# Paired output: operands of the pairs in a pool of their own, the prompt tile under the global scale, the output weights' work in ten steps, the last pair's gating on VectorE

## The chip, the cores and the metric

The kernel runs on one core of one Trainium2 chip. A core has a matrix engine (TensorE, PE in the profile, with its weight loads under PEld), three engines for elementwise work (VectorE or DVE, ScalarE or ACT, GpSimd or POOL) and a queue processor that only issues transfers (SyncE or SP); POOL and ACT can issue transfers too. Every engine works through its own instructions in order and waits on the others by semaphores. Matrix products land in PSUM, in banks of 128 partitions by 512 floats; everything else lies in SBUF. Sixteen DMA engines carry all transfers; the profile names their queues q1 (issued by SP), q0 (by POOL) and q10 (by ACT).

The metric is the device time of one execution in microseconds, the median of several runs.

## The reference

One layer of a mixer is applied to two groups of tokens, 2048 sample tokens and 128 prompt tokens, with the same weights and D_MODEL = 1024:

```python
proj = jnp.einsum('btd,de->bte', xn, w_in)
...
br = jnp.stack([o_a, o_b, o_c], axis=2)                  # three branches, 512 wide each
pb = jnp.einsum('btnw,nwd->btnd', br, w_branch)
gt = jax.nn.sigmoid(gates.reshape(B, T, N_BRANCH, D_MODEL))
merged = jnp.einsum('btnd,btnd->btd', gt, pb)
return jnp.einsum('btd,de->bte', merged, w_out), s_f, s_b
...
h = h + gate * out
y = rmsnorm(h, final_g)
```

`gates` is the last part of the input projection (three times 1024 columns). Branch A is a bidirectional gated DeltaNet, branch B a spatial gating unit, branch C a Fourier mixing. The change touches only what comes after the branches: the merge (the sigmoid gates times the branch projections, summed over the three branches), the output projection by `w_out`, the gated residual and the final norm.

## The kernel before, in words

All matrix products are made with pairs of float16 numbers: a float32 operand is scaled by a power of two and split into a high part (an ACT copy with a scale) and a low part (a DVE operation that subtracts the high part from the scaled source), and a product takes three matmuls, hi by hi, lo by hi, hi by lo. All 17 tiles of 128 tokens lie in SBUF as `xh` and `xl`, normed and transposed, through the whole kernel.

**The merges.** `merge` (L1682) is called three times, for the branches n = 1, 2 and 0. It loops over eight blocks of 128 output channels (`db`), over two halves of the tokens (1024 sample tokens; 1024 sample tokens and the 128 prompt tokens), and over tiles of 512 (or 128) tokens. A tile has 24 matmuls for the gate and 12 for the branch projection; ACT takes the sigmoid (`sg`, L1713), DVE multiplies it by the branch sum (L1722, or L1719 in the first merge), and POOL adds the result to a row `mrow` that SP loaded from DRAM (`mD`) and that is stored back afterwards. For n = 0 the halves run the other way round, so that the prompt tokens come third and the last tile of the last block holds sample tokens 512 to 1023.

Weights for these blocks are read by SP into a buffer `wst` (two buffers in all), and converted in three steps: a Square on ACT that gives a norm, a scale from it (a small matmul and a few DVE operations), and the split. `weight_step` (L379) takes one step of the next conversion or begins another; two steps after one has ended it issues the next read. In the kernel before it is called once per tile, through `pace.tick`. `getw(2, 2)` at the start of a block makes sure that the block's gate weight and branch weight are ready and allows two more. `gate_rows` (L1746) works between them, a chunk per half block from the fourth block of the second merge to the fourth of the third: it loads pieces of `w_ada` into the same two `wst` buffers and sums them on DVE (`ada_sum`, L466), for the row of residual gates in DRAM (`gateD`).

In the third merge the output weights are prepared as well (`out_w` (L1806), blocks 0 to 3; `out_step` takes two steps per tile), and from block 4 on `quarters` (L1843) turns each finished pair of rows, the one of block `db - 4` and the one of `db`, into seven split operands for the output stage, which POOL stores into DRAM (`paD`, L1858). All of these are split under one global scale `ms_s`, which stands before the third merge begins; its inverse is `ms_i`.

**The output stage.** Two sample tiles at a time (`two_tiles`, L1984) are multiplied by `w_out` with seven products instead of eight, from the seven operands (tile `pa`, 1.8 MB) and four prepared sums of weights (`tw`, 1 MB each, which SP loads into the place of `xl`). The prompt tile is done first and by itself (`one_tile`, L1957). In the kernel before its operand is prepared after the third merge's prompt tile of the last block: `ahead_out` calls `single` (L1873), which loads the whole prompt column of `mD`, takes its own Square and scale, and splits it into `whi` and `wlo`; the residual gates for the prompt are scaled by that scale and the weights' scales (`inv8`).

The buffers `bwp` (branch weights), `big` (the branch operand `o16` and `mrow`) are closed when the merges end, and the pool `op` of the output stage (two `pa` tiles, the sample's gate row `gb`, `final_g` and small things) lies in their place. A third `pa` tile lies in the pool `orp`. `next_pair` (L1922) issues the loads of `pa`. The rows of x for the residual are loaded into the place of `xh`.

Each pair's rows get gate, residual, Square with a row sum (ACT), the norm and the final scale, and are stored. The last pair (`end`) does this in pieces, so that less is left when the last matmul ends: pieces of 512, 384 and 128 columns, with row sums joined in `summed_up` (L2033) and two powers on POOL (L2065, L2066).

**Order.** The engines' order in this part is not written by hand. A planner lists the instructions of each engine by the times at which it believes them to be ready, and, where several are ready, by their place in the program; `tc.high_priority()` moves some ahead, `tc.issue_after` holds some back.

## Time and profile before

| | us |
|---|---|
| three runs | 2177.23, 2179.75, 2179.76 |
| median of the runs | 2179.75 |
| the profiled execution, its own time | 2178.41 |
| its span, first to last instruction | 2174.7 |
| PE busy | 2085.2 |
| third merge | from about 1725 to 1995 |
| prompt tile (`one_tile`) on PE | 1996 to 2011 |
| eight pairs on PE | 2015 to 2162 |
| end of the span | 2174.7 |

All times in the tables and rows are counted from the span's start. A row of the timeline has the start, the duration, the engine with the line of the kernel, the operation, what it writes and reads, and, in brackets, how long the engine stood idle before it and which instruction released it. A row of the waits has the waiting instruction, the one that it waited for, the sum in us, how many times, and the longest. The line is that of the innermost helper: all matmuls are recorded at L241, all output splits at L1803 (ACT) and L1804 (DVE), and the weights' splits at L317 and L318, so rows are told apart by their tiles. "SPq" and "POOL DMA_DIRECT2D" rows are issues of transfers; the bytes land later.

### The profile page before, as it was taken

The numbers are of one execution on the slowest core, as the hardware profiler recorded it, in microseconds if no ns is written. First come the engines' busy times: TensorE is split into PE (matmuls) and PEld (weight loads), VectorE is DVE, ScalarE is ACT, GpSimd is POOL, SyncE is SP. The second block draws the span as 40 slices with busy tenths as digits, with TensorE's granted clock in tenths as the row PEclk, the third lists the DMA queues.
The fourth block names the chain that finished last, engine by engine and source line by source line (L and its number), as shares of the span: only waits on it lengthen the run. The fifth ranks groups of instructions, "written<-read, shape, count | busy, mean of one in ns | idle before, by whom it ended". The sixth has DMA issues, their size and how long they took to land. (4 is left out here: it accounts for less than half of the span.)

```text
span 2174.7 us, 42636 instructions
## 1 busy us (share of the span) xinstructions
PE 2085.2 (96%) x16122; PEld 1191.9 (55%) x16122; DVE 1368.0 (63%) x3099; ACT 1061.8 (49%) x2454; POOL 761.9 (35%) x939
## 2 busy tenths in 40 slices
PE   7999999999899999999899999899999999999997
PEld 4455444465455677777465555555555544444443
DVE  6657744389778798457655556665563565566344
ACT  5554744476555664444544446655553443443111
POOL 0321332232433432443122223354533243343455
PEclk9999999999999999999999999999999999999999
DMA  9526732277776743444755455867665554557652
GB/s 349 217 75 198 253 121 81 88 235 219 239 231 211 231 146 91 140 140 117 232 167 162 161 172 181 251 212 220 201 203 158 165 193 135 182 201 267 255 218 102
DMA packets 222925, 403.36 MB, mean 185 GB/s; under 512 B 39720, under 2 KB 109888, under 8 KB 219904
## 3 DMA queue, kind: packets, MB, share of 16 engines
q1 hardware_dynamic: 167648, 290.65, 42.0%
q0 software_dynamic: 15248, 65.95, 8.3%
q10 hardware_dynamic: 39824, 44.05, 6.0%
q8 instruction: 126, 2.06, 0.4%
q14 instruction: 79, 0.65, 0.1%
HBM read 258.26 MB, written 142.30 MB: 184 GB/s over the span
## 5 line engine op out<-in xcount | busy, mean ns | idle before, releaser
L241 PE MATMUL b<-xh,whi 128*128 128x512 f16 (+1 forms) x1920 | 650.2, 348 | 4.0 <-DVE sg L1443 2.7
L241 PE MATMUL b<-xl,whi 128*128 128x512 f16 (+1 forms) x1920 | 651.0, 348 | 0.0
L241 PE MATMUL b<-xh,wlo 128*128 128x512 f16 (+1 forms) x1920 | 650.2, 348 | 0.0
L241 PEld LDWEIGHTS <-whi 128*128 128x128 f16 x3872 | 353.3, 98 | 328.4 <-issue 13.3
L241 PEld LDWEIGHTS <-wlo 128*128 128x128 f16 x1936 | 189.7, 98 | 179.5 <-DVE wlo L1804 3.1
L241 PE MATMUL b<-big,bhi 128*128 128x512 f16 (+1 forms) x960 | 250.8, 347 | 7.1 <-ACT big L1677 3.7
L241 PE MATMUL b<-big,blo 128*128 128x512 f16 (+1 forms) x480 | 163.0, 347 | 1.4 <-DVE blo L318 1.4
L1723 POOL TENSOR_TENSOR mrow<-mrow,sg 128x512 f32<-128x512 f32 (+1 forms) x80 | 92.2, 1153 | 146.9 <-DVE sg L1722 113.1
L241 PEld LDWEIGHTS <-xh 128*128 128x128 f16 x1496 | 117.1, 98 | 31.0 <-issue 2.3
L241 PEld LDWEIGHTS <-bhi 128*128 128x128 f16 x960 | 86.2, 98 | 83.6 <-issue 7.6
L943 POOL TENSOR_TENSOR cy<-cy,raw 128x545 f32<-128x545 f32 (+1 forms) x48 | 63.8, 1356 | 183.7 <-ACT raw L942 183.7
L241 PEld LDWEIGHTS <-pa 128*128 128x128 f16 x684 | 66.8, 98 | 83.8 <-ACT xh L1952 3.9
L1713 ACT ACTIVATE sg<-b,winv 128x512 f32<-128x512 f32 (+1 forms) x120 | 73.9, 616 | 66.1 <-PE b L241 65.3
L1177 POOL COPY T<-ES 32x256 f16<-32x256 f16 x68 | 29.2, 429 | 195.9 <-DMA ES<-ei 180.0
L241 PE MATMUL b<-whi,xh 128*128 128x128 f16 x544 | 92.9, 219 | 2.2 <-DVE yT L1629 1.4
L1722 DVE SCALAR_TENSOR_TENSOR sg<-b,binv,sg 128x512 f32<-128x512 f32 (+1 forms) x80 | 53.3, 666 | 63.1 <-PE b L241 58.3
L241 PE MATMUL b<-whi,xl 128*128 128x128 f16 x544 | 92.9, 219 | 0.0
L241 PE MATMUL b<-wlo,xh 128*128 128x128 f16 x544 | 92.9, 219 | 0.0
L318 DVE SCALAR_TENSOR_TENSOR wlo<-wst,wsc,whi 128x1024 f16<-128x1024 f32 x52 | 72.6, 1397 | 28.3 <-ACT whi L317 28.2
L305 ACT ACTIVATE wlo<-wst 128x1024 f16<-128x1024 f32 x52 | 55.0, 1058 | 68.2 <-DMA wst<-in_w_blk_dram 62.6
L241 PE MATMUL b<-xl,pa 128*128 128x512 f16 x384 | 86.8, 379 | 0.0
L1284 POOL TENSOR_TENSOR skn<-skn,ed 128x512 f32<-128x512 f32 x34 | 38.7, 1138 | 122.6 <-DMA skn<-kv 118.7
(512 smaller groups left out, 4312.8 us busy)
## 6 DMA issues: line engine op xcount, KB each, us to landing
wst<-in_w_blk_dram SPq DMA_DIRECT2D x58, 512.0 KB, 4.6
pa<-pa POOLq DMA_DIRECT2D x16, 896.0 KB, 4.3
pa<-pa SPq DMA_DIRECT2D x8, 1792.0 KB, 7.1
qkv<-cy POOLq DMA_DIRECT2D x12, 1089.0 KB, 5.2
st<-br SPq DMA_DIRECT2D x48, 256.0 KB, 3.2
mrow<-mrg SPq DMA_DIRECT2D x16, 576.0 KB, 4.2
dc<-dec SPq DMA_DIRECT2D x17, 512.0 KB, 5.0
kq<-qkv SPq DMA_DIRECT2D x34, 256.0 KB, 5.0
```

The source lines that it names most:

```text
L241: newest[0] = PE.matmul(out, l, r, start=start, stop=stop, skip_group_check=reopened)
L305: w.squared = A.activation(w.lo, st, AF.Square, accum_out=ss)
L318: w.low = V.scalar_tensor_tensor(w.lo, st, s, w.hi, ALU.mult, ALU.subtract)
L943: G.tensor_tensor(y[:, c0:c1], y[:, c0:c1], raw[:, 1 + c0:1 + c1], ALU.mult)
L1177: G.tensor_copy(T16[rows(a0, b), :, :, b], ES[0:32, :, 2 * a0 + b, :, wT])
L1284: G.tensor_tensor(h3(kn_), h3(kn_), bc(ed[:, d, t, :], P), ALU.mult)
L1713: gated_[0] = A.activation(sg, ps, AF.Sigmoid, scale=gw.inv)
L1722: V.scalar_tensor_tensor(sg, ps, binv[:, 1:2], sg, ALU.mult, ALU.mult)
L1723: G.tensor_tensor(mr, mr, sg, ALU.add)
```

## The change

1. `mrow` moves from the pool `big` to a pool `mrp` of its own, and the pairs' operands from `op` to a pool `opa` that is opened ahead of `op`.
2. `weight_step` is called once more per tile in all three merges.
3. `out_w` gets a further yield behind each of its two Squares, so that a block's preparation has ten steps after its load, two for each of the five tiles.
4. `single` goes away. At the start of the last block of the third merge `prompt_rows` loads seven of the eight row blocks of the prompt column from `mD` and splits them under the global scale `ms_s`; the eighth is split straight out of `mrow` when its tile is done, and no longer stored.
5. `ahead_out` multiplies the output weights' scales by `ms_i` once, scales the prompt's gates by them, and loads and scales the sample's gate row `gb` there too, into a `wst` buffer. Before, `gb` was loaded and scaled after the merges.
6. After the merges the first `next_pair` stands ahead of the loads of `tw` in the program.
7. In the last pair, DVE instead of POOL does the additions of the residual (three of them) and the gating of `p1`; `gated`, which the last pair no longer calls, uses POOL always; the row sums' small steps (`summed_up`) are put behind the last addition.

`halves` is renamed `as_pair`.

```diff
+    mrp = pool(ms_, "mrp", 2)
...
-                mrow = sb(big, [P, hn], "mrow", bufs=2)
+                mrow = sb(mrp, [P, hn], "mrow")
...
+                    if n == 0 and t0 == NS and db == KT - 1:
+                        as_pair(p16[0][:, db, :], p16[1][:, db, :], mr, ms_s)
+                    weight_step()
                     if step is not None:
                         step(db)
                     pace.tick(tn * MT)
...
-                if n or db < 4:
+                if n:
                     (SY if first else G).dma_start(mD[db][:, h0:h0 + hn], mrow)
-                elif h0:
+                elif db < 4:
+                    G.dma_start(mD[db][:, h0:h0 + hn], mrow)
+                elif h0 and db < KT - 1:
                     G.dma_start(mD[db][:, NS:NTOK], mrow[:, NS - h0:NTOK - h0])
...
                 A.activation(wlo[:, :, cols_[i]], sts[i], AF.Square, accum_out=ss[:, i:i + 1])
             yield
+            yield
...
-    def single(t, hl, pl, tag):
-        mt = sb(pl, [P, KT, P], tag, bufs=2)
-        SY.dma_start(mt, mD[:, :, t * P:(t + 1) * P].rearrange("k p t -> p k t"))
-        ss = sb(orp, [P, 1], "mss")
-        with tc.high_priority():
-            A.activation(hl[1], mt, AF.Square, accum_out=ss)
-            s, inv = scales(ss, orp, "msc")
-            halves(hl[0], hl[1], mt, s)
-        return hl, inv
...
+    def prompt_rows():
+        mt = sb(wp, [P, KT, P], "wst", bufs=2)[:, 0:KT - 1]
+        SY.dma_start(mt, mD[0:KT - 1, :, NS:NTOK].rearrange("k p t -> p k t"))
+        p16.extend(sb(wp, [P, KT, P], n_, F16, bufs=4) for n_ in ("whi", "wlo"))
+        as_pair(p16[0][:, 0:KT - 1], p16[1][:, 0:KT - 1], mt, ms_s)

     def ahead_out(h0):
         if h0:
-            pre.append(single(16, [sb(wp, [P, KT, P], n_, F16, bufs=4) for n_ in ("whi", "wlo")], wp, "wst"))
-            inv8 = sb(orp, [P, KT], "inv8")
-            V.tensor_scalar(inv8, winv, pre[0][1], None, ALU.mult)
+            for _ in weights_out:
+                pass
+            V.tensor_scalar(winv, winv, ms_i, None, ALU.mult)
             for i in range(2):
                 gp.append(sb(ep, [P, 512], "sg", bufs=4))
                 SY.dma_start(gp[i], gateD[1:2, i * 512:(i + 1) * 512].to_broadcast([P, 512]))
-                scale_gate(gp[i], gp[i], inv8[:, 4 * i:4 * i + 4])
+                scale_gate(gp[i], gp[i], winv[:, 4 * i:4 * i + 4])
+            gp.append(sb(wp, [P, D], "wst", bufs=2))
+            SY.dma_start(gp[2], gateD[0:1, :].to_broadcast([P, D]))
+            scale_gate(gp[2], gp[2], winv)
...
         if db == KT - 1:
             for _ in gates:
                 pass
+            while wsteps:
+                weight_step()
+            prompt_rows()
...
+    opa = pool(ctx, "opa", 2)
     op = pool(ctx, "op", 2)
...
-            ready.append(operands(orp, 1) if i % 3 == 2 else operands(op, 2))
+            ready.append(operands(orp, 1) if i % 3 == 2 else operands(opa, 2))
...
-    summed_in(1, 2)
     next_pair()
-    gb = sb(op, [P, D], "gb", bufs=1)
-    fg = sb(op, [P, D], "fg", bufs=1)
-    SY.dma_start(gb, gateD[0:1, :].to_broadcast([P, D]))
-    summed_in(0, 3)
+    for q in (1, 2, 0, 3):
+        SY.dma_start(tw[:, q].rearrange("p j l k c -> p j (l k c)"), tD[q])
...
-            (V if end else G).tensor_tensor(hh[j][:, cs], hh[j][:, cs], gb[:, cs], ALU.mult)
+            G.tensor_tensor(hh[j][:, cs], hh[j][:, cs], gb[:, cs], ALU.mult)
...
-        G.tensor_tensor(hh[0][:, left], hh[0][:, left], xr[0][:, left], ALU.add)
+        (V if end else G).tensor_tensor(hh[0][:, left], hh[0][:, left], xr[0][:, left], ALU.add)
...
+        def gate_add(out, src, gate, other):
+            V.tensor_tensor(out, src, gate, ALU.mult)
+            return V.tensor_tensor(out, out, other, ALU.add)
+
         total(u2, X, u2)
-        gated(1, right)
-        V.tensor_tensor(u2, u2, gb[:, right], ALU.mult)
-        G.tensor_tensor(u2, u2, xr[0][:, right], ALU.add)
-        G.tensor_tensor(p1, p1, gb[:, left], ALU.mult)
-        G.tensor_tensor(p1, p1, xr[1][:, left], ALU.add)
+        gate_add(p1, p1, gb[:, left], xr[1][:, left])
+        gate_add(hh[1][:, right], hh[1][:, right], gb[:, right], xr[1][:, right])
+        piece(1, 0, right, G)
+        gate_add(u2, u2, gb[:, right], xr[0][:, right])
+        piece(0, 0, left, G)
         product(Y, pa, 2, summed(3), False)
-        piece(1, 0, right, G)
-        piece(0, 0, left, G)
-        summed_up(1, 0)
-        summed_up(0, 0)
...
-        summed_up(1, 1)
-        summed_up(0, 1)
-        summed_up(0, 2)
+        with tc.issue_after(sooner.ins):
+            for j, i in ((1, 0), (0, 0), (1, 1), (0, 1), (0, 2)):
+                summed_up(j, i)
```

More of the change, by code (lines that the diff above doesn't have):

```diff
@@ L1800, in hybrid_flow_kernel, with as_pair @@
     tmp = sb(orp, [P, D], "sums")
-    def halves(hi, lo, src, s):
+    def as_pair(hi, lo, src, s):
         A.activation(hi, src, AF.Copy, scale=s)
@@ L1824, in out_w @@
             for q in q4:
-                halves(whi[:, q, cols_[i]], wlo[:, q, cols_[i]], sts[i][:, q], s)
+                as_pair(whi[:, q, cols_[i]], wlo[:, q, cols_[i]], sts[i][:, q], s)
             yield
@@ L1831, in out_w @@
             slot = slots[:, (4 * j + q) % 3]
-            halves(slot[:, 0], slot[:, 1], out, s)
+            as_pair(slot[:, 0], slot[:, 1], out, s)
             G.dma_start(tD[q, :, j, :], slot.rearrange("p l k c -> p (l k c)"))
@@ L1920, in hybrid_flow_kernel @@
     ready = []
+    gb, fg = gp[2], sb(op, [P, D], "fg", bufs=1)
     def next_pair():
@@ L1957, in one_tile @@
     def one_tile(t, prepared, xr, hh):
-        (mh, ml), inv = prepared
+        mh, ml = prepared
         for i in range(2):
@@ L2038, in summed_up @@
                 V.tensor_scalar(q_[:, 0:1], q_[:, 0:1], 1.0 / D, EPS, ALU.mult, ALU.add)
+        def gate_add(out, src, gate, other):
+            V.tensor_tensor(out, src, gate, ALU.mult)
+            return V.tensor_tensor(out, out, other, ALU.add)
         total(u2, X, u2)
-        gated(1, right)
-        V.tensor_tensor(u2, u2, gb[:, right], ALU.mult)
-        G.tensor_tensor(u2, u2, xr[0][:, right], ALU.add)
-        G.tensor_tensor(p1, p1, gb[:, left], ALU.mult)
-        G.tensor_tensor(p1, p1, xr[1][:, left], ALU.add)
+        gate_add(p1, p1, gb[:, left], xr[1][:, left])
[3 more added lines that the diff above has]
+        piece(0, 0, left, G)
         product(Y, pa, 2, summed(3), False)
-        piece(1, 0, right, G)
-        piece(0, 0, left, G)
-        summed_up(1, 0)
-        summed_up(0, 0)
         with tc.high_priority():
-            V.tensor_tensor(hh[1][:, left], Y, gb[:, left], ALU.mult)
-            sooner = V.tensor_tensor(hh[1][:, left], hh[1][:, left], p1, ALU.add)
+            sooner = gate_add(hh[1][:, left], Y, gb[:, left], p1)
             piece(1, 1, left, V)
@@ L2057, in two_tiles @@
             with tc.high_priority(), tc.issue_after(sooner.ins):
-                V.tensor_tensor(hh[0][:, cs], Z, gb[:, cs], ALU.mult)
-                V.tensor_tensor(hh[0][:, cs], hh[0][:, cs], u2[:, cs.start - 512:cs.stop - 512], ALU.add)
+                sooner = gate_add(hh[0][:, cs], Z, gb[:, cs], u2[:, cs.start - 512:cs.stop - 512])
                 piece(0, i, cs, V if i == 2 else G)
-        summed_up(1, 1)
-        summed_up(0, 1)
-        summed_up(0, 2)
+        with tc.issue_after(sooner.ins):
+            for j, i in ((1, 0), (0, 0), (1, 1), (0, 1), (0, 2)):
+                summed_up(j, i)
         norms = sb(op, [P, 2], "norms", bufs=1)
@@ L2077, in hybrid_flow_kernel @@
     next_pair()
-    one_tile(16, pre[0], xr[0], hh[0])
+    one_tile(16, p16, xr[0], hh[0])
     for i, t in enumerate(firsts):
```

13 lines of the change are left out of this document (4 added, 9 removed).

## The prediction

> **What bounds the kernel now.** I read the page's first part, then the list of TensorE's waits, then the timeline around each wait that the edits touch. The page first (share of the span, instructions):
>
> ```profile
> span 2174.7 us, 42636 instructions
> PE 2085.2 (96%) x16122; PEld 1191.9 (55%) x16122; DVE 1368.0 (63%) x3099; ACT 1061.8 (49%) x2454; POOL 761.9 (35%) x939
> ```
>
> TensorE (PE) is busy for 96%, and the change removes no matmul that matters, so it can win only idle PE time: 89.5 us in all, most of it in stages that it does not touch. The list of PE's waits (us in total, times, longest) shows what is within its reach:
>
> ```profile
> PE b L241 <- DMA pa<-pa: 3.5, 1, 3.5
> ...
> PE b L241 <- ACT sg L1713: 2.9, 2, 1.7
> ...
> PE b L241 <- DVE wlo L1804: 2.6, 1, 2.6
> ...
> PE b L241 <- DVE blo L318: 1.4, 2, 1.2
> ...
> PE b L241 <- ACT bhi L317: 0.6, 1, 0.6
> ```
>
> The first and third are the passage from the last merge to the output stage; the others are the merges. The rest is the tail behind the last matmul. I cost these three places apart.
>
> **The passage.** The timeline (start, us, what; idle before it and its releaser in brackets):
>
> ```profile
> 1994.93 0.38 PE L241 MATMUL b<-big,blo 128*128 128x512 f16 x1
> ...
> 1996.24 3.58 DVE L1804 SCALAR_TENSOR_TENSOR wlo<-wst,msc,whi 128x1024 f16<-128x1024 f32 x1
> 1996.26 0.39 PE L241 MATMUL b<-wohi,whi 128*128 128x512 f16 x1 [0.96 <-ACT whi L1803]
> ...
> 1999.88 0.39 PE L241 MATMUL b<-wohi,wlo 128*128 128x512 f16 x1 [2.58 <-DVE wlo L1804]
> ...
> 2010.86 0.38 PE L241 MATMUL b<-wohi,wlo 128*128 128x512 f16 x1
> 2014.72 0.59 PE L241 MATMUL b<-wohi,pa 128*128 128x512 f16 x1 [3.48 <-DMA pa<-pa]
> ```
>
> The merge ends at 1995.3. The prompt tile's 48 matmuls wait for its conversion (whi, wlo). The first pair then waits for its operands `pa` until 2014.72. The change converts the prompt tile inside the last block (seven eighths from DRAM, the last straight from the row, no Square and no scale of its own), so both waits go: 0.96 + 2.58. At the pitch between neighbouring 128x512 matmuls (1996.49 to 1996.71, 0.216) the 48 take 10.4 us, and PE reaches the first pair at 2005.7. That is worth something only if `pa` is there. Who held it, in SyncE's (SP's) waits and its timeline:
>
> ```profile
> SPq L1926 <- DVE sums L1853: 10.4, 1, 10.4
> ```
> ```profile
> 1992.18 1.06 SPq L1930 DMA_DIRECT2D xl<-tw  x2
> 2003.87 0.37 SPq L1926 DMA_DIRECT2D pa<-pa  x1
> ```
>
> SP sat for 10.4 us until the last reader of mrow was done, because `pa` lies in a pool over the merge's buffers. With mrow and `pa` in pools of their own only the last merge matmul (1995.3) holds it, and the issue moves from 2003.9 to about 1995.4. That looks like the whole 9 us. But the transfers ahead of it decide. Issues from 1988 to 1994 (KB each, median us to landing), then `pa`'s own, then the bytes that moved from 1988 to 2008.8 and from 1988 to 2013.2 (packets, MB, share):
>
> ```profile
> xl<-tw SPq DMA_DIRECT2D x4, 1024.0 KB, 14.4
> xh<-in_x_sample_dram SPq DMA_DIRECT2D x3, 512.0 KB, 4.9
> xh<-in_x_prompt_dram SPq DMA_DIRECT2D x1, 512.0 KB
> ```
> ```profile
> pa<-pa SPq DMA_DIRECT2D x1, 1792.0 KB, 10.7
> ```
> ```profile
> q1 hardware_dynamic: 1194, 6.32, 80.1%
> ```
> ```profile
> q1 hardware_dynamic: 1712, 8.15, 83.8%
> q0 software_dynamic: 258, 1.62, 16.6%
> ```
>
> Four weights of 1.049 MB and four rows of 0.524 MB make 6.29 MB on SP's queue ahead of `pa`; with its 1.835 MB, 8.13. The queue had moved 6.32 by 2008.8 and 8.15 by 2013.2, and `pa` landed 10.7 us after 2003.87, at 2014.6, 1.4 us behind its last byte: the queue works in order and `pa` waited for bandwidth. An issue 8.5 us earlier, behind the same eight transfers, gains nothing.
>
> Could `pa` go ahead of them? Their target (xl, xh) comes free with the last gate matmuls, some 2.6 us before the branch matmuls that now hold `pa`. SP's order follows readiness, not the program: the x rows, later in the program than the weights, are issued among them. I take `pa` as last of the nine again.
>
> So the landing is set by bytes. The prompt's 0.5 MB load and gate row gb leave the stretch; the former only shared the engines before 1988. GpSimd's (POOL's) queue q0 carries the stores of the merge, 0.92 MB each; of its 1.62 MB, 0.70 were a store still open at 1988, and I let a third of them, 0.23, move sooner. The merge's last store comes earlier too, since VectorE (DVE) no longer spends 3.58 us on wlo ahead of it. It is issued at 2009.88 today; by the distance between the first two of these rows it will start 7.6 us behind the last sg, which can follow the merge's end at 1995.6,
>
> ```profile
> 1987.62 0.75 DVE L1722 SCALAR_TENSOR_TENSOR sg<-b,binv,sg 128x512 f32<-128x512 f32 x1 [1.67 <-PE b L241]
> ...
> 1995.26 0.72 POOL L1858 DMA_DIRECT2D pa<-pa  x1 [5.55 <-DVE msc L270]
> ...
> 2009.88 0.75 POOL L1858 DMA_DIRECT2D pa<-pa  x1 [0.84 <-DVE pa L1804]
> ```
>
> so at 2003, and its 0.92 MB now shares the engines with what stands ahead of `pa`. Net +0.69 MB at 0.42 MB/us (below) is **+1.6 us** at the start of the pairs; bounds -0.6 (store late) and +2.2 (all of the store, nothing freed). PE waits about 10 us in one piece instead of three. After the old wait it ran at half clock,
>
> ```profile
> 2004.00:2014.00 10.00, 7.24 (x33) 3.05 (x31) 3.75 (x4) 1.76 (x3) 3.68 (x3) 0.98 1.02 423
> ...
> 2014.70:2018.10 3.40, 3.38 (x9) 1.23 (x10) 0.04 (x1) 0.00 (x0) 0.79 (x2) 0.51 1.01 420
> ```
>
> (us, busy time of PE, PEld, DVE, ACT, POOL, clock, DMA share, GB/s), 1.7 us lost, and will again: no change.
>
> **The conversion's new place.** The last block gets an ACT copy of 128x896 (about 1.0 us by the 1.15 of 1024), a DVE operation of up to 3.1 (7/8 of 3.58), a 128x128 pair, gb's load and its POOL scaling (1.9 us, from the pairs' start). They lie beside 33 us of matmuls with DVE idle for 12: nothing. Without that cover the 3.1 us of DVE would keep a finished sum in PSUM and PE waiting for the bank. On SP the prompt's load now stands ahead of the last block's row loads; it waits for the row store of the block before, which POOL issues half a block (some 16 us) earlier, so nothing queues behind it. It takes one wst buffer and gb the other, when no weight is left to read. The last prompt row's store to DRAM, the Square, three scale steps and one 1-column matmul fall away beside other work; the renamed helper costs nothing.
>
> **The merges.** A second weight step per tile makes a weight's three steps end within the third tile of a block; today the branch weight's last step falls into the next block, and PE waits: blo 1.4 and bhi 0.6, **-2.0 us**. The two sg waits are another matter:
>
> ```profile
> 1836.59 3.25 DVE L466 SCALAR_TENSOR_TENSOR sg<-wst,scT,sg 128x256 f32<-128x256 f32 x8 [4.79 <-DMA wst<-in_w_ada_dram]
> ...
> 1839.87 0.33 SPq L282 DMA_DIRECT2D wst<-in_w_brb_dram  x1
> ...
> 1842.47 0.63 ACT L305 ACTIVATE blo<-wst 128x512 f16<-128x512 f32 x1 [10.76 <-DMA wst<-in_w_brb_dram]
> ...
> 1843.82 0.27 PE L241 MATMUL b<-big,bhi 128*128 128x128 f16 x2 [1.70 <-ACT sg L1713]
> ```
>
> A gate chunk holds one of the two wst buffers, SP's load of the branch weight waits for it, ScalarE (ACT) stands 10.76 us in its Square, and the sigmoid behind it starves PE. The new steps read further ahead (three tiles instead of one or two), but through the same two buffers, so I leave these 2.9. Bounds: -4.9 (both groups gone), and above as the slow rival. The output weights' ten steps in five tiles instead of eight in four move ACT's, DVE's and POOL's work and POOL's stores one tile later; no wait of PE on them stands in the list, and the cover is 7.8 us of matmuls (36 at 0.216) in each tile. Without it a conversion of two 128x1024 weights, four ACT operations of 0.7, would stand ahead of a sigmoid.
>
> **The tail.** Rows of the last pair:
>
> ```profile
> 2156.77 0.68 DVE L2000 TENSOR_TENSOR xh<-b,st 128x512 f32<-128x512 f32 x1
> 2157.37 0.68 DVE L2000 TENSOR_TENSOR st<-b,st 128x512 f32<-128x512 f32 x1
> 2157.97 0.68 DVE L1995 TENSOR_TENSOR xh<-xh,gb 128x512 f32<-128x512 f32 x1
> 2158.56 1.76 DVE L2042 TENSOR_TENSOR st<-st,gb 128x512 f32<-128x512 f32 x1
> 2162.24 0.15 DVE L2038 TENSOR_SCALAR part<-part 128x1 f32<-128x1 f32 x1 [1.92 <-ACT xh L2030]
> ...
> 2166.58 0.28 DVE L2059 TENSOR_TENSOR xh<-xh,st 128x128 f32<-128x128 f32 x1
> ```
> ```profile
> 2158.06 1.71 POOL L2045 TENSOR_TENSOR sg<-sg,xh 128x512 f32<-128x512 f32 x1
> ...
> 2161.41 1.27 POOL L2031 TENSOR_TENSOR xh<-xh,fg 128x512 f32<-128x512 f32 x1
> ```
>
> DVE stood 1.92 us in a row-sum step behind POOL's additions; the change puts those additions on DVE and the row-sum steps last. DVE then has, from 2156.5, eleven 512-wide operations at the pitch of 0.60 (2156.77 to 2157.37), about 1.0 for the 384-wide pair and 0.5 for the 128-wide: 8.1 us, last addition at 2164.6 instead of 2166.86, -2.2. Against that stands POOL: three multiplications (1.27, 1.27, 1.04) remain, and DVE's operations stretch beside POOL (1.76 against 0.68). I take one such block of 1.2: **-1.0**; bounds -2.2 and, with all three, +1.4. The Trainium skill, page SBUF — State Buffer, section Who interferes with whom, says that a DVE instruction with two SBUF inputs contends with a GpSimd instruction that reads SBUF and that the loser fully blocks; the 1.76 agrees. By that rule all three can block, and the tail would be +1.4.
>
> **Sum.** +1.6 - 2.0 - 1.0 = -1.4 against the profiled execution's 2178.41: 2177.0. The three runs' median is 1.34 above that execution, so I forecast **2178**. Less than 0.2% (4.4 us) can't be told from no change.
>
> **Rivals.**
> *`pa` first.* If SP takes `pa` ahead of the weights, it lands near 2001 and PE runs through: -9.0 of idle, -1.7 of half clock, -3.0 of the rest: -13.7, 2166. For it: `pa` stands first in the new program text. Against: order by readiness.
> *Merges and tail at their best*: -4.9, -2.2, +1.6: -5.5, 2174.
> *Every POOL operation blocks in the tail*: +1.6 - 2.0 + 1.4 = +1.0, 2181. For it: the 1.76 ended 0.55 behind POOL's 1.71; against: the 0.68 at 2157.97 fell between two POOL operations and paid nothing.
> *Slower: ACT stands behind weight reads in every block that has a gate chunk.* Eight have one (four of the second merge, four of the third), two stall now at 1.15 and 1.70. Earlier Squares wait for the same buffers; six more at 1.4 are +8.4, in all +7.0: 2187. It decides from the fifth. For it: ACT's 10.76; against: reads lead by more.
>
> **Chances.** Forecast 0.45, `pa` first 0.10, merges and tail at best 0.19, POOL in the tail 0.08, slower rival 0.18. Faster 0.29, same 0.53, slower 0.18. The range 2170 to 2186 leaves out `pa` first and the top of the slow rival; the forecast alone has -4.8 (-0.6 - 2.0 - 2.2) to +1.6 (2.2 - 2.0 + 1.4), 2175 to 2181.
>
> **What would show it.** Right: no PE wait on whi or wlo at the passage; `pa` issued near 1995 yet landing some 18 us later, PE waiting about 10 us for it; no PE wait on blo or bhi; ACT's long brb waits still there; fewer microseconds between last matmul and end. Wrong: `pa` issued ahead of the weights, or new PE waits in the merges.

## The result, and the profile after

The changed kernel takes 2170.99 us (median of 8 runs, 2164.11 to 2173.97) against 2181.52 for the kernel before on the same chip: ratio 0.9946, 95% interval 0.9930 to 0.9963. (All ratios are estimated from all runs of a group and are not quotients of the two medians.) Beside the last experiments it was timed again: 2173.27 against 2178.78, ratio 0.9975, interval 0.9960 to 0.9989. So it is faster, by some 5 to 12 us; the forecast was 2178 and "no change". That 2170.99 lies just inside the range of 2170 to 2186 is luck: the fastest rival in that range stood at 2174. Two runs far out of line, 12445.25 us of e6 and 4413.44 us of the kernel before beside e5 to e8, are left out of the ratios.

The profiled execution after took 2164.11 us. It is the fastest of its eight: the first merge starts at 1033.1 in it, and between 1033.1 and 1046.2 in the profiled executions of the kernels below that run the same matmuls ahead of it (all but e10, e11 and e15); the changed kernel itself, profiled twice, has both ends of that range. Those microseconds belong to no edit, so the stages are compared by their length.

Before, by windows (from the first sigmoid of each merge to the next; the merge's end to the first pair's first matmul; the rest. Length, then the busy time of PE, PEld, DVE, ACT and POOL, PE's clock, DMA share, GB/s):

```profile
1037.50:1399.00 361.50, 346.37 (x3100) 205.33 (x3100) 215.87 (x556) 182.99 (x442) 95.61 (x144) 0.99 0.60 186
1399.00:1728.50 329.50, 325.65 (x2629) 186.12 (x2628) 187.40 (x489) 171.85 (x465) 140.15 (x164) 1.00 0.64 200
1728.50:1994.93 266.43, 261.10 (x1436) 126.67 (x1434) 160.65 (x341) 113.65 (x192) 101.91 (x110) 1.00 0.52 177
1994.93:2014.72 19.79, 12.78 (x51) 5.00 (x50) 11.09 (x16) 4.35 (x6) 8.40 (x8) 0.91 1.01 401
2014.72:2174.70 159.98, 146.84 (x684) 66.80 (x684) 67.80 (x94) 24.98 (x47) 84.93 (x75) 0.96 0.50 187
```

The same windows after:

```profile
1033.10:1389.50 356.40, 347.85 (x3108) 207.20 (x3108) 214.58 (x560) 184.68 (x445) 99.84 (x144) 0.99 0.61 190
1389.50:1720.10 330.60, 324.76 (x2620) 186.30 (x2619) 194.55 (x489) 170.98 (x465) 137.69 (x163) 0.99 0.63 198
1720.10:1981.73 261.63, 260.76 (x1435) 126.52 (x1433) 159.54 (x330) 111.71 (x185) 101.30 (x112) 1.00 0.52 179
1981.73:2002.22 20.49, 12.33 (x50) 5.03 (x49) 8.79 (x16) 6.03 (x9) 6.34 (x6) 0.86 1.02 422
2002.22:2162.30 160.08, 147.44 (x684) 66.94 (x684) 68.83 (x99) 25.18 (x49) 75.31 (x69) 0.96 0.49 186
```

The first merge is 5.1 us shorter, the second about 1 longer, the third 4.8 shorter; passage and pairs, at which five of the seven edits aim, are 0.7 and 0.1 longer. PE's idle time (length less busy) falls in the first merge from 15.1 to 8.6 us and in the third from 5.3 to 0.9. In the second it rises from 3.9 to 5.8: PE has a new wait of 3.0 us for a sigmoid at 1710.08 (1.4 us when the change was profiled again, e14). That sigmoid stood on ScalarE behind a copy that waited for the load of a branch's rows (`st` from `br`); new waits of PE in the merges were one of the signs of being wrong that the prediction named. ScalarE's waits for weight reads fall with PE's idle time. In the waits of the whole run (sum, times, longest), `blo` is written by the Square of a branch weight and `wlo` by that of a gate weight; before:

```profile
ACT wlo L305 <- DMA wst<-in_w_blk_dram: 62.6, 27, 6.8
ACT blo L305 <- DMA wst<-in_w_brb_dram: 56.3, 18, 10.8
```

and after:

```profile
ACT wlo L305 <- DMA wst<-in_w_blk_dram: 51.0, 25, 6.8
ACT blo L305 <- DMA wst<-in_w_brb_dram: 3.5, 2, 2.9
```

The waits for branch weights, which the forecast said would still be there, are all but gone. Of the two rows' sums some 28 to 29 us lie ahead of the first merge in both kernels; inside the merges they fall from 89.4 to 26.6 us.

### The profile page after: what moved, and what is told of

It reads as the page before. It is cut to its first block, busy times and chain, and to the rows that moved or that the text cites. A ratio compares the mean times of both kernels' runs of the same rounds, so it can differ in the third digit from the quotient of the medians.

```text
span 2162.3 us, 42634 instructions
## 1 busy us (share of the span) xinstructions
PE 2083.1 (96%) x16121; PEld 1193.1 (55%) x16121; DVE 1371.2 (63%) x3100; ACT 1062.1 (49%) x2453; POOL 753.1 (35%) x933
## 4 chain that ended last, share of the span: by engine, by line
PE 45%; DVE 7%; DMA 6%; issue 2%; ACT 2%; POOL 1%; SPq 0%; POOLq 0%; DVEq 0%; ACTq 0%
PE b L241 44%; DMA st<-br 2%; DMA pa<-pa 1%; DMA wst<-in_w_ada_dram 1%; DVE XB L1103 1%; DVE E L1104 1%; DMA ei<-XB 1%; DVE big L1679 0%; DVE wlo L318 0%; DMA N<-n 0%; ACT big L1678 0%; POOL o L1359 0%; DVE S L1332 0%; DVE sg L466 0%; DVE o L1237 0%
## 5 line engine op out<-in xcount | busy, mean ns | idle before, releaser
L241 PEld LDWEIGHTS <-whi 128*128 128x128 f16 x3872 | 352.5, 98 | 327.6 <-issue 13.1
L1723 DVE SCALAR_TENSOR_TENSOR sg<-b,binv,sg 128x512 f32<-128x512 f32 (+1 forms) x80 | 53.4, 667 | 62.5 <-PE b L241 58.3
L318 DVE SCALAR_TENSOR_TENSOR wlo<-wst,wsc,whi 128x1024 f16<-128x1024 f32 x52 | 68.1, 1311 | 28.0 <-ACT whi L317 26.6
L317 ACT ACTIVATE whi<-wst,wsc 128x1024 f16<-128x1024 f32 x52 | 59.5, 1145 | 49.5 <-DVE wsc L269 47.5
```

The costliest lines, as they stand in the source:

```text
L241: newest[0] = PE.matmul(out, l, r, start=start, stop=stop, skip_group_check=reopened)
L317: w.made = A.activation(w.hi, st, AF.Copy, scale=s)
L318: w.low = V.scalar_tensor_tensor(w.lo, st, s, w.hi, ALU.mult, ALU.subtract)
L1723: V.scalar_tensor_tensor(sg, ps, binv[:, 1:2], sg, ALU.mult, ALU.mult)
```

## The experiments

The stages of the profiled executions (us, cut as above) and the times against the kernel before on the same chip. There are four groups, each on a chip of its own: e1 to e4, e5 to e8, e9 to e12, e13 to e15. The first theory was that the gain is the second weight step's, through reads that lead by more; the rivals were that the steps move the conversions, and that passage or tail had gained after all.

| kernel | first, second, third merge | passage | rest | median | ratio (95%) |
|---|---|---|---|---|---|
| before | 361.5, 329.6, 266.4 | 19.8 | 160.0 | | |
| changed | 356.4, 330.5, 261.6 | 20.5 | 160.1 | 2170.99 | 0.9946 (0.9930 to 0.9963) |
| e1 before + second step | 357.5, 330.3, 262.9 | 21.0 | 160.6 | 2173.45 | 0.9973 (0.9958 to 0.9988) |
| e2 changed without second step | 362.2, 330.1, 270.2 | 22.9 | 160.3 | 2188.51 | 1.0037 (1.0020 to 1.0053) |
| e3 changed, `pa` first | 358.3, 330.2, 261.6 | 12.8 | 161.6 | 2163.73 | 0.9930 (0.9908 to 0.9953) |
| e4 before + last pair | 362.5, 329.0, 265.0 | 21.2 | 160.7 | 2179.80 | 1.0001 (0.9985 to 1.0017) |
| e5 before, reads sooner | 359.8, 337.9, 260.3 | 20.6 | 160.6 | 2182.82 | 1.0011 (0.9994 to 1.0027) |
| e6 e1, reads held | 359.2, 333.3, 263.9 | 20.3 | 160.9 | 2174.64 | 0.9971 (0.9958 to 0.9984) |
| e7 before + ten steps | 362.1, 330.6, 270.8 | 22.0 | 160.5 | 2184.58 | 1.0026 (1.0012 to 1.0040) |
| e8 changed, eight steps | 357.3, 329.5, 265.5 | 20.5 | 159.5 | 2175.12 | 0.9982 (0.9970 to 0.9994) |
| e9 e3, x4 copy later | 356.4, 333.3, 261.0 | 12.1 | 158.6 | 2160.96 | 0.9920 (0.9899 to 0.9942) |
| e10 before, Squares held | 355.8, 331.0, 260.2 | 21.8 | 160.7 | 2171.46 | 0.9976 (0.9960 to 0.9993) |
| e11 e9, Squares held | 354.7, 334.3, 260.2 | 10.7 | 157.9 | 2155.47 | 0.9898 (0.9876 to 0.9920) |
| e12 changed, no POOL in the tail | 357.5, 331.4, 262.2 | 20.4 | 159.7 | 2173.42 | 0.9973 (0.9955 to 0.9990) |
| e13 before + second step + ten steps | 355.4, 332.3, 261.4 | 20.8 | 160.4 | 2173.12 | 0.9970 (0.9954 to 0.9986) |
| e14 the changed kernel again | 357.5, 329.6, 260.9 | 20.6 | 160.0 | 2173.27 | 0.9975 (0.9960 to 0.9989) |
| e15 e11 + the tail of e12 | 355.6, 331.8, 260.2 | 11.3 | 157.7 | 2152.89 | 0.9889 (0.9865 to 0.9913) |

Each row's stages are those of one execution; the change's two rows (changed, e14) differ by up to 1.1 us in a stage. In e10, e11 and e15 the first sigmoid comes 14 or 15 matmuls sooner, so that their first merge is counted too long. From one and the same matmul shortly before it to the second merge's first sigmoid it is 365.3 us before, 360.3 in the changed kernel and in e9, 356.9 in e10, 355.8 in e11 and 356.7 in e15.

**Which edit: e1, e2, e4.** Before with the second step alone, the change without it, and before with the new last pair alone.

```diff
 (e1, one more per tile)
+                    weight_step()
 (e2, the changed kernel)
-                    weight_step()
```

> The kernel before with one edit: the second weight step per tile in the three merges. Theory A (the merges' gain is the second step: reads and conversions end earlier, so ACT no longer stands in a Square for a read): 7 to 11 us faster than before, the third merge about 5 us shorter (its four waits of 1.15, 1.22, 1.70 and 1.26 gone), the passage unchanged (19.4 us from the merge's last matmul to the first pair). Theory B (the gain is the passage and what the planner makes of the other edits): within 3 us of before. My recorded step said 2.0 us faster.

> The changed kernel without the second weight step. Theory A: it loses the merges' gain, within 3 us of before (2176 to 2182 against a before of 2179). Theory B: it keeps 7 us or more of the gain. Both: the passage stays bound by bytes, about 20 us from the merge's last matmul to the first pair.

> The kernel before with the last pair's edit alone (additions on DVE, row sums last). By the trace of the changed kernel the time from the first pair's first matmul to the end is 160.1 us against 160.0: no gain, within 1 us of before. My recorded step said 1.0 us faster, the skill's rule with all three blocks 1.4 us slower.

The step alone gives 0.9973 and a first merge of 357.5, a little less than the 7 to 11 us expected; without it the rest of the change is slower than before (1.0037), which neither theory had, with a third merge of 270.2; the last pair's edit moves nothing that the times can tell. The gain is the second step's.

**Why the step helps: e5, e6, e10.** e5 asks for a read as soon as a weight's steps are done, without a second step; e6 has the step but sends both reads in the last tile; e10 has neither, and only holds each Square behind the sigmoid of its own tile.

```diff
 (e5, inside the merges)
-                wlate[0] = 2
+                while len(wread) < min(len(wdone) - len(wsteps) + 2, len(wlist)):
+                    read_next()
 (e6, inside the merges)
-                wlate[0] = 2
+                wlate[0] = 0
...
+                    while tile == 5 and len(wread) < min(len(wdone) - len(wsteps) + 2, len(wlist)):
+                        read_next()
+                    weight_step()
 (e10)
-        w.squared = A.activation(w.lo, st, AF.Square, accum_out=ss)
+        with tc.issue_after(gate_now[0].ins) if gate_now[0] else ExitStack():
+            w.squared = A.activation(w.lo, st, AF.Square, accum_out=ss)
...
-                        gated_[0] = A.activation(sg, ps, AF.Sigmoid, scale=gw.inv)
+                        gate_now[0] = gated_[0] = A.activation(sg, ps, AF.Sigmoid, scale=gw.inv)
```

> The kernel before with one edit: inside the merges the reads of the next weights go out as soon as a weight's three steps are done (gate weight at the third tile, branch weight at the start of a block), so that each read leads its Square by three tiles, as with the second step; the conversion itself keeps its place (one step a tile). Theory A (what the second step gains is the reads' lead): ScalarE's waits on the weight reads in the first merge fall from 32 to about 10 us, the first merge shortens by about 4.5 us, the third by about 3, ratio 0.997. Theory B (the gain is that the conversion is spread otherwise, its last operations no longer in the next block): the first merge stays near 361.5 us, ratio 0.999 to 1.001, at most the 2.0 us of waits on blo and bhi move.

> The kernel before with the second weight step per tile, but with the reads held back to the last tile of each block (both weights' reads), so that the gate read leads its Square by one tile and the branch read by two, as before the change. Theory A (the reads' lead): ScalarE's waits on the reads stay near 30 us in the first merge, which stays near 361.5 us, and the ratio is 0.999 to 1.002. Theory B (the place of the conversion): first merge near 357 us, ratio 0.997, as with the whole second step.

> The kernel before with one edit: in the merges a weight's Square is held behind the sigmoid of the tile in which the program calls for it. No second step. Theory F (without the second step ScalarE's order puts each Square right behind a read that went out only when the split before it freed a buffer, and ScalarE's standing there is what costs): ScalarE's waits on the reads fall below 5 us in the first merge, the first merge takes 356 to 358 us instead of 361.5, ratio about 0.997. Rival D (the gain of the second step is that the splits come earlier, whatever the Squares wait for): first merge stays at 361 us or longer, ratio 1.000 or above, since held Squares make the splits no earlier.

The first theory fell: sooner reads gain nothing (1.0011), and with reads put late in the program the step keeps its gain by the times (0.9971; the first merge of 359.2 us lies between the two expectations, the time and the waits below do not). The one profiled execution of e6 does not show that gain: its three merges take 956.4 us together against 957.5 before, with one wait of PE of 4.2 us for a sigmoid in the second. In e5 the third merge is 6.1 us shorter and the second 8.3 longer, together 598.2 us against 596.0; in the second, two waits of PE for `sg` by DVE are new (2.29 and 1.86 us), and ahead of the first of them DVE itself had stood 4.46 us for the Square of a gate weight. The timeline of the first merge says why the reads do not matter. Before, around one branch weight:

```profile
1213.03 0.75 DVE L318 SCALAR_TENSOR_TENSOR blo<-wst,wsc,bhi 128x512 f16<-128x512 f32 x1
1213.81 0.33 SPq L282 DMA_DIRECT2D wst<-in_w_brb_dram  x1
1218.25 0.63 ACT L305 ACTIVATE blo<-wst 128x512 f16<-128x512 f32 x1 [1.13 <-DMA wst<-in_w_brb_dram]
```

and in e1:

```profile
1201.87 0.74 DVE L318 SCALAR_TENSOR_TENSOR blo<-wst,wsc,bhi 128x512 f16<-128x512 f32 x1
1202.64 0.33 SPq L282 DMA_DIRECT2D wst<-in_w_brb_dram  x1
1210.56 0.63 ACT L305 ACTIVATE blo<-wst 128x512 f16<-128x512 f32 x1 [0.30 <-PE b L241]
```

In both the read leaves at once when the split before it (DVE's `blo`, ending 1213.78 and 1202.61) frees one of the two `wst` buffers; in e5 and e6, too, most reads of the first merge leave within 0.2 us of the end of the split before them, wherever the program asks for them. What differs is ScalarE's order. Before, ScalarE comes to the next Square 3.3 us behind that read's issue and stands 1.13 us until it has landed; the sigmoids and the DeltaNet scan's work of this stage stand behind it. In e1 the Square starts 7.9 us behind the read and does not wait for it. The waits for reads over the whole run, e5:

```profile
ACT wlo L305 <- DMA wst<-in_w_blk_dram: 76.6, 28, 8.0
ACT blo L305 <- DMA wst<-in_w_brb_dram: 35.6, 17, 5.2
```

e6:

```profile
ACT wlo L305 <- DMA wst<-in_w_blk_dram: 57.6, 25, 6.8
ACT blo L305 <- DMA wst<-in_w_brb_dram: 4.4, 2, 3.0
```

e10, the only such row left but one of 0.4 us:

```profile
ACT wlo L306 <- DMA wst<-in_w_blk_dram: 24.1, 8, 6.8
```

e10 tests this alone: the Squares keep the kernel's old number of steps and only stand later. Its first merge has no wait on a read left, and the ratio is 0.9976, like the second step's 0.9973. That is the cost shown by itself. The 24.1 us left lie all ahead of the first merge; inside the merges ScalarE's waits for weight reads fall from 89.4 us to 0.4, and the three merges by 10.5 (957.5 to 947.0; 13.2 from the same matmul). By the times the gain is smaller, 0.24%, some 5 us; the profiled execution of e10 is the fastest of its twelve.

**The ten steps: e7, e8, e13.** Before with ten steps alone, the change with eight, and before with second step and ten steps, nothing else.

```diff
 (e7, e13: added; e8: taken away)
                 A.activation(wlo[:, :, cols_[i]], sts[i], AF.Square, accum_out=ss[:, i:i + 1])
             yield
+            yield
```

> The kernel before with the output weights' work in ten steps a block instead of eight, and nothing else. Theory C (the ten steps cost the third merge what the second weight step then hides): third merge 4 us longer (270 instead of 266.4 us), ratio 1.002. Prediction's own view (off TensorE's path, nothing): third merge 265 to 267 us, ratio 0.999 to 1.001.

> The changed kernel with the output weights' work put back to eight steps a block. Theory C (ten steps cost, and the second weight step only covers a part): third merge 258 to 260 us instead of 261.6, ratio 0.992 to 0.994. Rival (with the second weight step the ten steps are what lets the third merge gain 5 us more than with the step alone): third merge back to 263 to 266 us, ratio 0.996 to 0.997.

> The kernel before with the second weight step and the ten steps a block, and nothing of the rest (no pools, no prompt tile under the global scale, no new last pair). Theory H (the whole gain is in the merges, and these two edits make it together: either alone leaves a wait in the two blocks with a gate chunk, ScalarE's standing or VectorE's sums): first merge 357, third merge 261 to 263 us, ratio 0.994 to 0.996, as the whole change. Rival I (the step alone has the gain of the merges, the rest comes from the passage and the other edits): ratio 0.997 as the step alone.

Alone the ten steps cost 0.26%. The block of the third merge with the last gate chunk (db 3), by windows, before:

```profile
1828.95:1866.59 37.64, 34.72 (x188) 16.46 (x187) 21.73 (x47) 15.12 (x27) 14.21 (x16) 1.00 0.46 151
```

in e7:

```profile
1837.16:1878.41 41.25, 37.58 (x188) 17.23 (x187) 19.46 (x44) 14.55 (x26) 12.44 (x14) 0.92 0.40 132
```

in e8:

```profile
1830.11:1868.21 38.10, 36.05 (x188) 16.86 (x187) 21.86 (x45) 14.84 (x25) 16.47 (x18) 0.96 0.44 150
```

and after:

```profile
1819.75:1854.48 34.73, 34.36 (x188) 16.41 (x187) 19.99 (x45) 14.51 (x25) 12.93 (x14) 1.00 0.46 146
```

The same block with its 188 matmuls takes 37.64 us before and 41.25, 38.10 and 34.73 in the three others. Of e7's 3.6 us over the kernel before, 2.9 are PE's busy time at a clock of 0.92 instead of 1.00: most of what the ten steps cost there is the slower clock behind the waits. In e7 ScalarE stands in a Square behind the gate chunk's buffer, as before the change, and PE waits for the sigmoid:

```profile
1848.36 0.63 ACT L305 ACTIVATE blo<-wst 128x512 f16<-128x512 f32 x1 [4.74 <-DMA wst<-in_w_brb_dram]
1851.54 0.27 PE L241 MATMUL b<-big,bhi 128*128 128x128 f16 x2 [2.69 <-ACT sg L1713]
```

In e8 ScalarE is free and DVE is what is late: it stands for the chunk, and the product that empties PE's bank (`sg`, L1723) stands behind its sums:

```profile
1841.77 2.07 DVE L466 SCALAR_TENSOR_TENSOR sg<-wst,scT,sg 128x256 f32<-128x256 f32 x5 [5.13 <-DMA wst<-in_w_ada_dram]
1844.55 0.38 PE L241 MATMUL b<-xh,whi 128*128 128x512 f16 x1 [2.05 <-DVE sg L1723]
```

e8's third merge of 265.5 us is what the rival expected, its ratio of 0.9982 worse than either expectation. With both edits (changed, e13, e14) this wait is 0.2 to 0.5 us and the third merge 260.9 to 261.6. By time, though, e13 gives 0.9970, the share of the step alone: the expectation that the pair would make 0.994 to 0.996 was not met, and e14, the whole change again, gives 0.9975 beside it. So by the times the two edits are the whole change, and whether the change is faster than e8 (0.9982, in another group) they can't tell. Left open is why the first ratio was 0.9946: the stages of the change agree within 1.1 us in its two profiled executions, so the difference lies with the chip or the runs and not with an edit.

**The passage: e3 and e9.** e3 holds the loads of `tw` behind `pa` on SP; e9 also puts, in `quarters`, the copy of the older row (x4) behind that of the new row (x8).

```diff
 (e3)
+        with tc.issue_after(sent.ins):
+            sent = SY.dma_start(tw[:, q].rearrange("p j l k c -> p j (l k c)"), tD[q])
 (e9)
+        r = as_pair(T7[:, :, 0, 1:3], T7[:, :, 1, 1:3], x8, ms_s)
+        with tc.issue_after(r.ins):
+            as_pair(T7[:, :, 0, 0], T7[:, :, 1, 0], x4[:, :, 0], ms_s)
```

> The changed kernel with the four loads of tw held behind the load of the first pair's operands on SP's queue. Theory A (the queue works in order and the operands waited for the bytes ahead of them): the operands land 6 to 8 us after their issue instead of 19.9, PE's wait of 5.3 us for them goes, the pairs start 8 to 10 us sooner behind the merge, and the kernel is 8 to 10 us faster than the changed one, some 20 us faster than before. Rival (the landing is bound by something else, or the weights tw now come too late): the pairs start at most 3 us sooner.

> The changed kernel with the first pair's operands sent ahead of the output weights (as in the run before it with that edit) and, in the quarters of the third merge, ScalarE's copy of the older row's operands (x4) held behind that of the new row (x8). Theory E (ScalarE stands some 10 us in the x4 copy for POOL's store of the same buffer, and the sigmoid and the prompt's copies behind it starve TensorE): the two waits of 2.0 and 2.3 us in the passage shrink, passage 10.8 to 11.5 us instead of 12.8, ratio 0.991 to 0.992. Rival (the x8 copy waits for the same store and stands there instead): passage 12.5 to 13 us, ratio 0.993 as before.

The passage after the change (timeline; then the transfers issued in it, KB each and us to landing, two of those from 1970 on):

```profile
1975.40 0.75 POOL L1865 DMA_DIRECT2D pa<-pa  x1 [4.31 <-DVE pa L1810]
1982.14 0.37 SPq L1937 DMA_DIRECT2D pa<-pa  x1
1985.29 0.51 ACT L1809 ACTIVATE pa<-st,msc 128x256 f16<-128x256 f32 x1 [10.45 <-issue]
1990.16 0.58 PE L241 MATMUL b<-wohi,whi 128*128 128x512 f16 x1 [2.87 <-ACT sg L1714]
2002.22 0.58 PE L241 MATMUL b<-wohi,pa 128*128 128x512 f16 x1 [5.30 <-DMA pa<-pa]
```
```profile
pa<-pa SPq DMA_DIRECT2D x2, 1792.0 KB, 19.9
```
```profile
pa<-pa POOLq DMA_DIRECT2D x1, 896.0 KB, 9.8
```

`pa` is issued 0.4 us behind the start of the last merge matmul, as forecast, and takes 19.9 us. ScalarE stands 10.45 us in the x4 copy, which starts 0.1 us behind the landing of POOL's store of 1975.40 (the profile names no releaser here; the copy of this kind at 1963.13 names the landing of such a store, and in e3 the copy at 1991.37 starts 0.1 us behind one, too); behind it stand the sigmoid and the prompt's last copies, and PE waits 2.87 us inside the prompt tile. In e3:

```profile
1989.07 0.38 SPq L1937 DMA_DIRECT2D pa<-pa  x1
1989.54 2.11 SPq L1942 DMA_DIRECT2D xl<-tw  x4
1991.37 0.51 ACT L1809 ACTIVATE pa<-st,msc 128x256 f16<-128x256 f32 x1 [9.61 <-issue]
1996.24 0.38 PE L241 MATMUL b<-wohi,whi 128*128 128x512 f16 x1 [2.03 <-ACT sg L1714]
```

The pairs start straight after the prompt tile and the passage falls to 12.8 us: the bytes ahead of `pa` were what held it. The 7.7 us are a little less than the 8 to 10 expected. e9 takes the x4 copy's standing away as well; the passage is 12.1, with a wait of 1.4 us for `pa` in its place, and not the expected 10.8 to 11.5.

**The tail: e12, and the change again, e14.**

```diff
 (e12)
-        piece(1, 0, right, G)
+        piece(1, 0, right, V)
...
-        piece(0, 0, left, G)
+        piece(0, 0, left, V)
...
-                piece(0, i, cs, V if i == 2 else G)
+                piece(0, i, cs, V)
```

> The changed kernel with the last pair's three remaining multiplications by the final gain moved from POOL to VectorE. Theory G (each of them stretches the VectorE operation beside it: 1.76, 1.04 and 1.05 us for operations of 0.68, 0.68 and 0.28, 2.2 us in all): the stretched operations are gone, VectorE gains 2.2 us and takes on about 1.7, so that from the last matmul to the end it is 12.0 to 12.4 us instead of 12.6. Rival (the stretches are not POOL's doing and stay): 14 us or more. The time itself changes by less than the runs can tell: ratio 0.993 to 0.996.

> The changed kernel itself, beside the others on one chip, since its copy with another last pair came out at 0.9973 against its own 0.9946 although its tail was 0.6 us shorter. If that difference was one between chips, the changed kernel comes out between 0.994 and 0.997 here; if the last pair's edit cost something that the profile hides, at 0.9946 or below and e15 above it is not as fast as 0.9898.

The tail after the change, POOL's three multiplications and the DVE operations beside them:

```profile
2147.26 1.34 POOL L2033 TENSOR_TENSOR xh<-xh,fg 128x512 f32<-128x512 f32 x1 [4.12 <-DMA out_dram<-xh]
2147.38 1.76 DVE L2043 TENSOR_TENSOR st<-st,wst 128x512 f32<-128x512 f32 x1
2149.82 1.65 POOL L2033 TENSOR_TENSOR xh<-xh,fg 128x512 f32<-128x512 f32 x1 [1.23 <-DVE xh L2044]
2150.98 1.04 DVE L2044 TENSOR_TENSOR xh<-xh,sg 128x512 f32<-128x512 f32 x1
2153.70 0.99 POOL L2033 TENSOR_TENSOR xh<-xh,fg 128x384 f32<-128x384 f32 x1 [2.23 <-DVE xh L2044]
2153.79 1.05 DVE L2044 TENSOR_TENSOR xh<-xh,st 128x128 f32<-128x128 f32 x1
```

The same operations of e12, without POOL:

```profile
2152.33 0.68 DVE L2043 TENSOR_TENSOR st<-st,wst 128x512 f32<-128x512 f32 x1
2156.05 0.69 DVE L2044 TENSOR_TENSOR xh<-xh,sg 128x512 f32<-128x512 f32 x1
2158.86 0.28 DVE L2044 TENSOR_TENSOR xh<-xh,st 128x128 f32<-128x128 f32 x1
```

All three blocked: 1.08 + 0.35 + 0.77 = 2.2 us. The end follows the last matmul by 12.6 us after the change, 12.0 in e12, 13.1 before. Over all profiled executions it is 12.8 to 13.7 us with the old last pair, 12.2 to 12.7 with the new one, and 11.8 and 12.0 without POOL (e15, e12). e12's ratio of 0.9973 is like the change's 0.9975 in e14; 0.6 us can't be told by times.

**Together: e11 and e15.**

> The changed kernel with the operands first, the x4 copy later and the Squares held behind their tile's sigmoid. Theory F: ScalarE's waits left in the merges (9 us in the first, 15 in the second) go too, first merge 352 to 355 us, ratio 0.989 to 0.990. Rival: the second step has taken all that there was, ratio as with the operands first alone, 0.992 to 0.993.

> The changed kernel with all edits that helped: operands first, x4 copy later, Squares held, and the last pair's multiplications by the final gain on VectorE. If the last pair's edit is worth the 0.6 us that its profile shows, 0.989 to 0.990; if it costs 5 us, 0.992.

`pa` first, the x4 copy later and the Squares held (e11) make 2155.47, ratio 0.9898, better than e9's 0.9920 though the intervals overlap; with e12's tail (e15) 2152.89, ratio 0.9889, 0.9865 to 0.9913, the best version found. Both the ratio and the first merge of 354.7 us are as expected. In sum the merges of e11 look no shorter than those of the change (949.2 against 948.5), but that is the sooner first sigmoid: from the same matmul they take 950.3 us, against 952.4 in the change and 954.5 in e9, whose second merge was as long (333.3, and 334.3 in e11). Its passage of 10.7 is the 48 matmuls and nothing else, and the pairs take 157.9 instead of 160.1: PE runs into them without a wait, and its clock is 1.00 from 1996.4 to 2010.0.

## Why the prediction was wrong, step by step

The step that failed is the merges' term, -2.0 with a lower bound of -4.9. In the profiled executions that have the second step with free reads and unheld Squares the first merge takes 355.4 to 358.3 us, without it 361.5 to 362.5; the merges together go from 957.5 to 948.5, -9.0, and in e14 to 948.0. The third merge's 4.8 us are nearly all of what the term's lower bound allowed for all three; the first merge's 5.1 us stood at 0.8 (blo 0.2, bhi 0.6) in the term. Two sentences of the prediction led there.

- PE's other idle time lies "in stages that it does not touch". The first merge's idle time was put down by line to the scan (S, R and o by ScalarE) and taken as the scan's own. These are the waits that shrink, since ScalarE, which feeds both scan and merge, had stood in Squares. PE's three longest in the first merge before, and what is left of the first after:

```profile
PE b L241 <- ACT S L1220: 5.9, 4, 2.2
PE b L241 <- ACT big L1677: 3.7, 2, 2.3
PE b L241 <- ACT R L1192: 2.3, 3, 1.2
```
```profile
PE b L241 <- ACT S L1220: 2.2, 1, 2.2
```

  `big` falls to 1.4, and `R` is no longer among the waits. Only waits labelled with the weight itself (`blo`, `bhi`) were counted, 2.0 of the 24.3 us that PE idled in the merges.
- The new steps read further ahead, "but through the same two buffers, so I leave these 2.9". The first half is right: the buffers set the read, not the program's read step (e5, e6). The conclusion was wrong, since the distance from read to Square, not the read, decided. So the forecast that ScalarE's long waits on branch reads stay was wrong (56.3 to 3.5 us). In the third merge both `sg` waits, 2.9, went as well as `blo` and `bhi`; 0.8 us of waits on `sg` by DVE is left.

The other points:

- **Passage**, +1.6 within -0.6 to +2.2: measured +0.7 in the profile. The mechanism held: `pa` issued at the merge's end, nearly 20 us to landing, no wait on `whi` or `wlo`. PE's idle came in two pieces (2.87 and 5.30) instead of the one of 10, the first from ScalarE behind POOL's store, which the prediction had not seen.
- **Half clock unchanged**: after the 5.30 us PE had a clock of 0.50 from 2002.2 to 2005.7, as forecast. The prediction counted one such stretch; each kernel has two, the other being 0.63 from 1999.88 to 2004.00 before (behind the wait of 2.58) and 0.66 from 1990.1 to 1994.5 after (behind the 2.87).
- **Ten steps, nothing**: wrong by themselves (e7, +0.26%), right with the second step as far as the times can tell (0.9970 in e13, 0.9973 in e1).
- **Tail**, -1.0: measured -0.5 from last matmul to end, and none of it left in the sum from the pairs' start (160.0 and 160.1). Its direction was right and one assumption wrong: three POOL operations blocked, not one. The Trainium skill, page SBUF — State Buffer, section Who interferes with whom, says that VectorE with two SBUF inputs and a reading GpSimd shut each other out; the rows of the tail agree with it in all three places, and e12 confirms it by taking POOL away. By that rule I had put the tail at +1.4, at three blocks of 1.2 us; they cost 2.2 together, which against the -2.2 of the moved work leaves 0.0.
- **`pa` first** (2166): it did not happen by itself, and e3 made it happen. The passage fell by 7.7 us against the change, not by the 12.3 between that rival and the forecast: a wait behind ScalarE's standing (2.03) and one on a copy in the first pair (2.28) took 4.3 us, and the half clock came all the same (0.59 from 2009.05), so that the rest grew by 1.5.
- **The slower rival**, ScalarE behind weight reads in the gate chunk's blocks: not in the change, but it is part of what happens to the edits without the second step (e2 and e7, 270 us in the third merge).

With the measured terms the forecast's sum would have been -9.0 + 0.7 + 0.1, about -8 us or 0.9962, between the two measured ratios.

## What to carry to other kernels

A long wait on an engine that feeds the bottleneck is charged in the profile to whatever stood behind it, so count the whole queue behind it, not only the waits that carry its name. When a transfer's issue follows the release of a buffer, moving the request in the program gains nothing (e5); move the consumer away from the issue, or free the buffer sooner. An edit that spreads work can cost by itself and be free beside another edit, so test edits alone and together before pricing them by addition.

## What was not expected of the hardware

A wait of about 2 us can cost PE its clock. In e8 PE stood for 2.05 us; then its clock, by windows (length, PE's busy time, clock, DMA share, GB/s):

```profile
1844.55:1847.00 2.45, 2.45 (x8) 0.63 0.00 0
1847.00:1850.00 3.00, 3.00 (x12) 0.73 0.67 215
1850.00:1853.00 3.00, 3.00 (x16) 1.00 0.50 202
```

About 1.7 us are lost behind it (36.05 us busy in that block against 34.36). Yet the 2.03 us in e3's passage, and the 1.70 us in the kernel before, were followed by a clock of 1.00 (1996.24 to 1999.00, and the block from 1828.95). So near 2 us it falls out either way; what decides was not found.

POOL's store of 0.9 MB landed in 4.1 us when it was issued at 1965.99 and in 9.8 us when it was issued at 1975.40 among the eight transfers that SP issued from 1975.02 on: by its landing, 0.1 us ahead of the copy, that store, off every list of PE's waits, is what held ScalarE.
